# Adaptive max pooling on one core: 63 consecutive rows for each partition, a nine-row ring, 48 KB load runs and 9 KB store runs

## The chip, the cores and the metric

One core of a Trainium2 chip; no other core of it ran. The metric is the device time of one execution in microseconds (us). "Before" is the kernel before the change, "changed" the kernel after it. The profiled span is about 2 us shorter than the reported time (336.9 against 339 for before). "Packet records" are the start, duration and size of every DMA packet, as the trace holds them.

## The reference

32 x 256 rows of 4096 floats (134.2 MB) become 32 x 256 rows of 256 floats (8.4 MB). As 4096 is a multiple of 256, each output is the maximum of 16 neighbours.

```python
for i in range(output_size):                       # 256
    start = int(i * length / output_size)          # 16 i
    end = int((i + 1) * length / output_size)
    result[:, :, i] = np.max(x[:, :, start:end], axis=-1)
```

## The kernel before

There are 8192 rows, 64 for each of the 128 partitions. Tile `n` takes 256 consecutive rows, two for each partition, so a partition reads one run of 32 KB and the next partition's run follows directly. Three such tiles rotate. SyncE issues the loads, VectorE reduces, ScalarE issues the first stores, and the last 16 stores of the body are held back and put on SyncE's queue between and behind the last loads.

```python
xt = xf.rearrange("(n p r) (o w) -> n p r o w", p=P, r=R, w=W)   # R = 2
ot = of.rearrange("(n p r) m -> n p (r m)", p=P, r=R)
...
for n in range(n_body):                                          # 30
    t = in_pool.tile([P, R, O, W], fp32, tag="in")               # bufs=3
    nc.sync.dma_start(out=t, in_=xt[n])                          # 4 MB, 32 KB a partition
    o = new_out()
    for r in range(R):
        nc.vector.reduce_max(out=o[:, r * O : (r + 1) * O], in_=t[:, r], ...)
    out_tiles[n] = o
    if n >= defer_start:
        deferred.append(n)                                       # held back
    else:
        nc.scalar.dma_start(out=ot[n], in_=o)                    # 256 KB, 2 KB a partition
...  # two rows loaded whole, two rows in four pieces of 4 KB a partition, held stores in between
```

Of the kernel before, what the change touches and what calls it, by code (L numbers as in the profile page):

```python
# [1 line left out]

# [4 lines left out]


@with_exitstack  # L10
def kernel(
    ctx: ExitStack,
    tc: tile.TileContext,
    x: bass.AP,
    output_size: bass.AP,
    out: bass.AP,
):
    nc = tc.nc

    B, C, L = x.shape  # L20
    O = int(output_size)
    assert L % O == 0, (L, O)
    W = L // O

    P = nc.NUM_PARTITIONS

    xf = x.flatten_outer_dims()
    of = out.flatten_outer_dims()
    rows = xf.shape[0]
    assert rows % P == 0  # L30

    fp32 = mybir.dt.float32

    R = 2
    IN_BUFS = 3
    CHUNKS_PER_ROW = 4
    N_CHUNK_ROWS = 2
    N_FULL_ROWS = 2
    DEF_A = 6
    DEF_B = 5  # L40
    DEF_C = 5

    while R > 1 and rows % (P * R) != 0:
        R //= 2
    nprow = rows // P
    nmacro = nprow // R
    n_chunks = CHUNKS_PER_ROW if O % CHUNKS_PER_ROW == 0 else 1
    oc = O // n_chunks

    n_tail_prow = min(N_CHUNK_ROWS + N_FULL_ROWS, nprow)  # L50
    n_chunk_prow = min(N_CHUNK_ROWS, n_tail_prow)
    n_tail_macro = -(-n_tail_prow // R)
    n_body = nmacro - n_tail_macro
    tail_start_prow = n_body * R
    n_defer = min(DEF_A + DEF_B + DEF_C, max(n_body - 1, 0))

    xt = xf.rearrange("(n p r) (o w) -> n p r o w", p=P, r=R, w=W)
    ot = of.rearrange("(n p r) m -> n p (r m)", p=P, r=R)

    in_pool = ctx.enter_context(tc.tile_pool(name="inpool", bufs=IN_BUFS))  # L60
    out_pool = ctx.enter_context(
        tc.tile_pool(name="outpool", bufs=min(nmacro, n_defer + 5))
    )

    out_tiles = {}
    deferred: list[int] = []

    def new_out():
        return out_pool.tile([P, R * O], fp32, tag="out", name="o")

    def emit_deferred(k):
        for _ in range(k):
            if deferred:
                m = deferred.pop(0)
                nc.sync.dma_start(out=ot[m], in_=out_tiles[m])  # L75

    defer_start = n_body - n_defer
    for n in range(n_body):
        t = in_pool.tile([P, R, O, W], fp32, tag="in")
        nc.sync.dma_start(out=t, in_=xt[n])  # L80
        o = new_out()
        for r in range(R):
            nc.vector.reduce_max(  # L83
                out=o[:, r * O : (r + 1) * O],
                in_=t[:, r],
                axis=mybir.AxisListType.X,
            )
        out_tiles[n] = o
        if n >= defer_start:
            deferred.append(n)  # L90
        else:
            nc.scalar.dma_start(out=ot[n], in_=o)

    emit_deferred(DEF_A)

    o = None
    last_n = nmacro - 1
    for q in range(tail_start_prow, nprow):
        n, r = divmod(q, R)
        if r == 0 or o is None:  # L100
            o = new_out()
            out_tiles[n] = o
        if q == nprow - n_chunk_prow:
            emit_deferred(DEF_B)
        if q < nprow - n_chunk_prow:
            tr = in_pool.tile([P, 1, O, W], fp32, tag="inrow", bufs=2)
            nc.sync.dma_start(out=tr, in_=xt[n][:, r : r + 1])
            nc.vector.reduce_max(  # L108
                out=o[:, r * O : (r + 1) * O],
                in_=tr[:, 0],  # L110
                axis=mybir.AxisListType.X,
            )
        else:
            for c in range(n_chunks):
                tl = in_pool.tile(
                    [P, oc, W], fp32, tag="inchunk", bufs=2 * n_chunks
                )
                nc.sync.dma_start(
                    out=tl, in_=xt[n][:, r, c * oc : (c + 1) * oc, :]
                )  # L120
                nc.vector.reduce_max(  # L121
                    out=o[:, r * O + c * oc : r * O + (c + 1) * oc],
                    in_=tl,
                    axis=mybir.AxisListType.X,
                )
        if r == R - 1 and n != last_n:
            nc.scalar.dma_start(out=ot[n], in_=o)

    emit_deferred(len(deferred))

    nc.scalar.dma_start(out=ot[last_n], in_=out_tiles[last_n])


# [1 line left out]
_INS = ['x', 'output_size']  # L135
_OUTS = [((32, 256, 256), 'float32')]
#: Inputs that are plain numbers.
_NUMBERS = {'output_size': 256}


# [26 lines left out]
```

## Time and profile before

| What | Before | Where it is read |
|---|---|---|
| time, median of 3 first runs | 339.17 us | runs |
| span | 336.9 us | page |
| VectorE busy | 281.0 us, 83% | page, part 1 |
| bytes moved | 142.6 MB | page, parts 2 and 3 |
| DMA share from 20 to 280 us | 1.00 to 1.01 | windows |
| one row reduced | 4.41 us | groups of instructions |

From the page of before, its lines on VectorE, on the DMA engines (busy tenths in 40 slices, then GB/s of each slice), on packets and on the queues (q1 is SyncE's, q10 ScalarE's):

```profile
span 336.9 us, 241 instructions
...
DVE 281.0 (83%) x70; POOL 0.2 (0%) x4
...
DMA  7999999999999999999999999999999999999997
GB/s 311 436 436 441 417 454 406 454 409 454 426 430 430 436 428 434 430 430 435 429 438 432 436 432 436 436 436 428 424 436 428 436 412 436 429 414 427 405 414 275
DMA packets 10370, 142.63 MB, mean 423 GB/s; under 512 B 1152, under 2 KB 1152, under 8 KB 6272
...
q1 hardware_dynamic: 8064, 138.42, 96.1%
q10 hardware_dynamic: 2304, 4.20, 3.2%
```

The 1152 packets under 512 B are 4-byte ones, 16 for each of the 72 DMAs, which report that a DMA is done; they are called semaphore packets below. The DMA line stands at nine tenths or more in every slice but the first and the last. VectorE is well used too, but not all the time.

Two stretches of before in the windows view. The columns are the stretch, its length, VectorE's busy time with its instruction count, GpSimd's, the TensorE clock, the DMA share and GB/s:

```profile
core 0: us, DVE busy (x) POOL busy (x), PEclk, DMA share, GB/s
20.00:160.00 140.00, 118.67 (x28) 0.00 (x0) 1.00 1.01 431
185.00:280.00 95.00, 85.25 (x21) 0.00 (x0) 1.00 1.00 431
```

A DMA share of 1.00 means that the 16 engines had, as good as always, a packet in hand. It can read more, for two reasons: the view adds up whole packets that start in the stretch, and a packet overlaps the next one slightly. With the packets clipped to the stretch the two shares are 1.006 and 1.003.

The group of whole-row reduces of before (busy us, mean ns of one, then the idle time in front of them and who ended it):

```profile
L83 DVE TENSOR_REDUCE o<-t 128x256 f32<-128x4096 f32 x60 | 262.4, 4414 | 50.5 <-DMA t<-in_x_dram 50.5
```

And a piece of before's chain of waits, with its shares by line (start us, length us, what):

```profile
by line: DMA t<-in_x_dram 60.0%; DVE o L83 23.4%; DMA out_dram<-o 10.7%; DMA tl<-in_x_dram 2.8%; DVE o L121 0.7%; SPq L75 0.5%; SPq L80 0.3%; issue 0.3%; DVEq L83 0.0%
...
64.09 8.76 DVE o L83 x2
72.85 0.02 issue
72.87 22.19 DMA t<-in_x_dram
```

The chain gives VectorE 24% of the span. It is easy to read this as "a quarter of the time is compute on the critical path". It isn't: the load that follows a reduce was free to be issued only when the reduce freed its buffer, but two other loads were still outstanding at that moment, and the DMA engines did not run dry. The 22 us that the chain shows for a load of 4 MB is more than twice what 4 MB takes at 431 GB/s (9.7 us): the rest is waiting in the queue.

### The profile page before, as it was taken

To read this page: it belongs to the slowest core of one execution; us is meant where nothing else is said; L and a number is where in the kernel's file an instruction comes from. 1 tells how busy PE (TensorE), PEld (TensorE's weight loads), DVE (VectorE), ACT (ScalarE), POOL (GpSimd) and SP (SyncE) were. 2 spreads that over 40 slices of the span, in tenths; PEclk is the share of its full clock that TensorE was granted. 3 is DMA by queue.
4 is the path that set the end of the run, shared out by engine and by line. 5 is a ranking of instruction groups with operands and counts; after the bars stand their busy time and mean duration, and the time that the engine had idled before them with its cause. 6 is when DMAs were issued, how large, how long until landed. Compare 5 with 4: busy or idle time off the path is not lost.

```text
span 336.9 us, 241 instructions
## 1 busy us (share of the span) xinstructions
DVE 281.0 (83%) x70; POOL 0.2 (0%) x4
## 2 busy tenths in 40 slices
DVE  0488988888988889888899888888988888898895
POOL 0000000000000000000000000000000000000000
DMA  7999999999999999999999999999999999999997
GB/s 311 436 436 441 417 454 406 454 409 454 426 430 430 436 428 434 430 430 435 429 438 432 436 432 436 436 436 428 424 436 428 436 412 436 429 414 427 405 414 275
DMA packets 10370, 142.63 MB, mean 423 GB/s; under 512 B 1152, under 2 KB 1152, under 8 KB 6272
## 3 DMA queue, kind: packets, MB, share of 16 engines
q1 hardware_dynamic: 8064, 138.42, 96.1%
q10 hardware_dynamic: 2304, 4.20, 3.2%
q14 instruction: 2, 0.02, 0.0%
HBM read 134.22 MB, written 8.39 MB: 423 GB/s over the span
## 4 chain that ended last, share of the span: by engine, by line
DMA 74%; DVE 24%; SPq 1%; issue 0%; DVEq 0%
DMA t<-in_x_dram 60%; DVE o L83 23%; DMA out_dram<-o 11%; DMA tl<-in_x_dram 3%; DVE o L121 1%; SPq L75 1%; SPq L80 0%; DVEq L83 0%
## 5 line engine op out<-in xcount | busy, mean ns | idle before, releaser
L83 DVE TENSOR_REDUCE o<-t 128x256 f32<-128x4096 f32 x60 | 262.4, 4414 | 50.5 <-DMA t<-in_x_dram 50.5
L121 DVE TENSOR_REDUCE o<-tl 128x64 f32<-128x1024 f32 x8 | 9.8, 1220 | 1.0 <-DMA tl<-in_x_dram 0.6
L108 DVE TENSOR_REDUCE o<-tr 128x256 f32<-128x4096 f32 x2 | 8.8, 4420 | 1.0 <-DMA tr<-in_x_dram 0.9
L148 POOL MEMSET const-bfloat16-1.0<- 128x1 bf16 x1 | 0.1, 102 | 0.0
L148 POOL MEMSET const-uint8-127<- 128x1 uint8 x1 | 0.1, 101 | 0.0
L148 POOL MEMSET const-float32-0.0<- 128x1 f32 x1 | 0.1, 99 | 0.2 <-issue 0.2
L148 POOL MEMSET const-float32-1.0<- 128x1 f32 x1 | 0.1, 98 | 0.0
## 6 DMA issues: line engine op xcount, KB each, us to landing
t<-in_x_dram SPq DMA_DIRECT2D x30, 4096.0 KB, 21.5
out_dram<-o ACTq DMA_DIRECT2D x16, 256.0 KB, 16.1
out_dram<-o SPq DMA_DIRECT2D x16, 256.0 KB, 14.0
tr<-in_x_dram SPq DMA_DIRECT2D x2, 2048.0 KB, 16.4
tl<-in_x_dram SPq DMA_DIRECT2D x8, 512.0 KB, 9.2
```

Source lines behind the costliest of these rows:

```text
L75: nc.sync.dma_start(out=ot[m], in_=out_tiles[m])
L83: nc.vector.reduce_max(out=o[:, r * O : (r + 1) * O], in_=t[:, r], axis=mybir.AxisListType.X,)
L108: nc.vector.reduce_max(out=o[:, r * O : (r + 1) * O], in_=tr[:, 0], axis=mybir.AxisListType.X,)
L121: nc.vector.reduce_max(out=o[:, r * O + c * oc : r * O + (c + 1) * oc], in_=tl, axis=mybir.AxisListType.X,)
L148: nc = _bacc.Bacc("TRN2", target_bir_lowering=False, num_devices=1)
```

## The change

Its intent is longer runs and fewer packets. Each partition owns 63 consecutive rows; with three rows a load it reads runs of 48 KB, and with nine rows a store it writes runs of 9 KB. The price is that neighbouring partitions now read 63 x 16 KB = 1008 KB apart. The last 128 rows, one for each partition, are handled at the end. A ring of nine rows takes the place of three two-row buffers.

```diff
-    R = 2
-    IN_BUFS = 3
...
+    RING = 9
+    G = 63
+    STORE = 9
+    LOAD = 3
+    LATE = [3, 2, 2, 1, 1]
+    HELD = 4
+    PIECES = 4
...
-    xt = xf.rearrange("(n p r) (o w) -> n p r o w", p=P, r=R, w=W)
-    ot = of.rearrange("(n p r) m -> n p (r m)", p=P, r=R)
...
+    main = G * P
+    xg = xf[0:main].rearrange("(p s r) (o w) -> s p r o w", p=P, r=STORE, w=W)
+    og = of[0:main].rearrange("(p s r) m -> s p (r m)", p=P, r=STORE)
+    xl = xf[main:rows].rearrange("p (o w) -> p o w", w=W)
+    ol = of[main:rows]
...
+    for g in range(G // STORE):
+        o = outs[g % len(outs)]
+        sizes = LATE if g == G // STORE - 1 else [LOAD] * (STORE // LOAD)
+        r = 0
+        for n in sizes:
+            at = n_read % RING
+            nc.sync.dma_start(out=ring[:, at : at + n], in_=xg[g][:, r : r + n])
+            for i in range(n):
                 nc.vector.reduce_max(
-                    out=o[:, r * O + c * oc : r * O + (c + 1) * oc],
-                    in_=tl,
+                    out=o[:, (r + i) * O : (r + i + 1) * O],
+                    in_=ring[:, at + i],
                     axis=mybir.AxisListType.X,
                 )
+            n_read += n
+            r += n
+        if g < G // STORE - 1 - HELD:
+            nc.scalar.dma_start(out=og[g], in_=o)
+        else:
+            held.append((og[g], o))
...  # the last row in PIECES loads and reduces
+    for dst, src in held:
+        nc.sync.dma_start(out=dst, in_=src)
+    nc.scalar.dma_start(out=ol, in_=last_out)
```

More of the change, by code (lines that the diff above doesn't have):

```diff
@@ L18 @@
     nc = tc.nc
+    P = nc.NUM_PARTITIONS
+    fp32 = mybir.dt.float32
     B, C, L = x.shape
@@ L23 @@
     W = L // O
-    P = nc.NUM_PARTITIONS
     xf = x.flatten_outer_dims()
@@ L29 @@
     rows = xf.shape[0]
-    assert rows % P == 0
-    fp32 = mybir.dt.float32
-    R = 2
-    IN_BUFS = 3
-    CHUNKS_PER_ROW = 4
-    N_CHUNK_ROWS = 2
-    N_FULL_ROWS = 2
-    DEF_A = 6
-    DEF_B = 5
-    DEF_C = 5
-    while R > 1 and rows % (P * R) != 0:
-        R //= 2
-    nprow = rows // P
-    nmacro = nprow // R
-    n_chunks = CHUNKS_PER_ROW if O % CHUNKS_PER_ROW == 0 else 1
-    oc = O // n_chunks
-    n_tail_prow = min(N_CHUNK_ROWS + N_FULL_ROWS, nprow)
-    n_chunk_prow = min(N_CHUNK_ROWS, n_tail_prow)
@@ L52 @@
-    n_tail_macro = -(-n_tail_prow // R)
-    n_body = nmacro - n_tail_macro
-    tail_start_prow = n_body * R
-    n_defer = min(DEF_A + DEF_B + DEF_C, max(n_body - 1, 0))
-    xt = xf.rearrange("(n p r) (o w) -> n p r o w", p=P, r=R, w=W)
-    ot = of.rearrange("(n p r) m -> n p (r m)", p=P, r=R)
-    in_pool = ctx.enter_context(tc.tile_pool(name="inpool", bufs=IN_BUFS))
-    out_pool = ctx.enter_context(
-        tc.tile_pool(name="outpool", bufs=min(nmacro, n_defer + 5))
-    )
-    out_tiles = {}
@@ L66 @@
-    deferred: list[int] = []
-    def new_out():
-        return out_pool.tile([P, R * O], fp32, tag="out", name="o")
-    def emit_deferred(k):
-        for _ in range(k):
-            if deferred:
-                m = deferred.pop(0)
-                nc.sync.dma_start(out=ot[m], in_=out_tiles[m])
-    defer_start = n_body - n_defer
-    for n in range(n_body):
-        t = in_pool.tile([P, R, O, W], fp32, tag="in")
-        nc.sync.dma_start(out=t, in_=xt[n])
-        o = new_out()
-        for r in range(R):
-            nc.vector.reduce_max(
-                out=o[:, r * O : (r + 1) * O],
-                in_=t[:, r],
-                axis=mybir.AxisListType.X,
-            )
-        out_tiles[n] = o
-        if n >= defer_start:
-            deferred.append(n)
-        else:
-            nc.scalar.dma_start(out=ot[n], in_=o)
@@ L94 @@
-    emit_deferred(DEF_A)
-    o = None
-    last_n = nmacro - 1
-    for q in range(tail_start_prow, nprow):
-        n, r = divmod(q, R)
-        if r == 0 or o is None:
-            o = new_out()
-            out_tiles[n] = o
-        if q == nprow - n_chunk_prow:
-            emit_deferred(DEF_B)
-        if q < nprow - n_chunk_prow:
-            tr = in_pool.tile([P, 1, O, W], fp32, tag="inrow", bufs=2)
-            nc.sync.dma_start(out=tr, in_=xt[n][:, r : r + 1])
-            nc.vector.reduce_max(
-                out=o[:, r * O : (r + 1) * O],
-                in_=tr[:, 0],
-                axis=mybir.AxisListType.X,
-            )
-        else:
-            for c in range(n_chunks):
-                tl = in_pool.tile(
-                    [P, oc, W], fp32, tag="inchunk", bufs=2 * n_chunks
-                )
-                nc.sync.dma_start(
-                    out=tl, in_=xt[n][:, r, c * oc : (c + 1) * oc, :]
-                )
+    assert rows == 64 * P
@@ new lines @@
+    RING = 9
[5 more added lines that the diff above has]
+    PIECES = 4
+    pool = ctx.enter_context(tc.tile_pool(name="pool", bufs=1))
+    ring = pool.tile([P, RING, O, W], fp32, tag="ring", name="ring")
+    outs = [
+        pool.tile([P, STORE * O], fp32, tag=f"out{i}", name=f"out{i}")
+        for i in range(G // STORE - 1)
+    ]
+    last_out = pool.tile([P, O], fp32, tag="lastout", name="lastout")
+    main = G * P
+    xg = xf[0:main].rearrange("(p s r) (o w) -> s p r o w", p=P, r=STORE, w=W)
@@ new lines @@
+    og = of[0:main].rearrange("(p s r) m -> s p (r m)", p=P, r=STORE)
+    xl = xf[main:rows].rearrange("p (o w) -> p o w", w=W)
+    ol = of[main:rows]
+    n_read = 0
+    held = []
+    for g in range(G // STORE):
[6 more added lines that the diff above has]
+            for i in range(n):
@@ L121 @@
                 nc.vector.reduce_max(
-                    out=o[:, r * O + c * oc : r * O + (c + 1) * oc],
-                    in_=tl,
+                    out=o[:, (r + i) * O : (r + i + 1) * O],
+                    in_=ring[:, at + i],
                     axis=mybir.AxisListType.X,
                 )
-        if r == R - 1 and n != last_n:
-            nc.scalar.dma_start(out=ot[n], in_=o)
-    emit_deferred(len(deferred))
-    nc.scalar.dma_start(out=ot[last_n], in_=out_tiles[last_n])
+            n_read += n
@@ new lines @@
+            r += n
[3 more added lines that the diff above has]
+            held.append((og[g], o))
+    at = n_read % RING
+    oc = O // PIECES
+    for c in range(PIECES):
+        cut = slice(c * oc, (c + 1) * oc)
+        nc.sync.dma_start(out=ring[:, at, cut], in_=xl[:, cut])
+        nc.vector.reduce_max(
+            out=last_out[:, cut], in_=ring[:, at, cut], axis=mybir.AxisListType.X
+        )
+    for dst, src in held:
+        nc.sync.dma_start(out=dst, in_=src)
```

## The prediction

> **What bounds the kernel now.** The memory traffic, and nothing else. The profile's page gives a span of 336.9 us in which the DMA engines are busy in nine tenths or more of every slice but the first and last; its DMA queues moved 142.6 MB (134.2 MB read, 8.4 MB written, as they must be). The windows view shows a DMA share of 1.00 to 1.01 from 20 to 280 us, at 431 GB/s. The Trainium skill, "DMA: Bandwidth & Descriptors", section "Where 436 GB/s comes from", states 435.2 GB/s as the ceiling of the 16 ports; the trace agrees, it runs 1% below. VectorE is busy 281 us (83%): its wait in front of the loads (50.5 us) is slack, not cost. The chain of waits alternates 22 us of load and 8.76 us of reduce, but that is the buffer loop closing behind a full queue: in the packet records the first packet starts about 2 us after the span's start, the last ends about 1 us before its end, and all 16 engines are busy between, except some 1.3 us of imbalance in the last 5 us.
>
> So the floor of any rearrangement is about 142.6 MB / 435.2 GB/s = 327.7 us (an estimate from that page), plus 3 us of start and end and 2.3 us between span and reported time: 333 us. Over 2% faster (below 332.4 us) isn't there.
>
> **What the change does.** The arithmetic is the same: 62 whole-row reduces of 4.41 us become 63, eight quarter-row ones of 1.22 us become four. The ring is three slots of three rows instead of three of two, still triple buffering. Loads: 3840 packets of 32 KB become 2432 of 48 KB (plus 256 of 32 KB); 1024 pieces of 4 KB become 512. Stores: 4096 packets of 2 KB become 896 of 9 KB and 128 of 1 KB. 72 DMAs become 35, so 1152 semaphore packets become 560.
>
> Costs, read from the trace: loads alone ran at 432.4 GB/s (185 to 280 us), loads with 2 KB stores at 431.7, and the small-packet end at 386 to 420. Above pure payload a 32 KB packet costs about 2 to 4 ns and a 2 KB packet about 5 (80 ns start to start, against 75). Per engine I estimate: stores 256 x 5 ns shrink to a quarter, -0.9 us; long loads -0.2 us; 4 KB pieces -0.1 us; semaphores 37 x 9 ns, -0.3 us. All of it is on the critical path, since the queue is it. Sum -1.5 us; a slightly better end could give 0.5 more.
>
> Will the queue stay full? A slot of three rows is freed 13.2 us after it lands, a load lasts about 14.6 us, and another whole load is queued: yes. At the end, VectorE finishes about 10.6 us after the last load, but four held stores (10.9 us) and the fifth cover it.
>
> **The row pitch.** Partitions now lie 1008 KB apart, not 32 KB. The same page, section "Latency and other measured facts", reports losses for large power-of-two pitches and none once padded by 4 KiB. 1008 KB is no power of two, so I expect no loss. No run here has shown it.
>
> **Prediction.** 337.4 us, 80% range 335.6 to 341. Faster by over 2%: 0.01; within: 0.88; slower: 0.11.
>
> **Right if**: DMA share stays 1.00 in the middle at 431 to 434 GB/s; packets near 5040; VectorE's mean per row stays 4.41 us; no idle DMA in the last 15 us.
>
> **Wrong if**: the long pitch makes 48 KB packets last over 1.82 us (then GB/s in mid-span falls, evenly); the held stores fail to cover VectorE's end (idle DMA near the end); or engines drift apart and end unevenly.

## The result, and the profile after

The changed kernel took 336.94 us (median of 4 runs, 336.87 to 337.29) beside 338.95 for before: ratio 0.9941, 95% interval 0.9925 to 0.9957. Two more series gave 0.9954 and 0.9945. The mean of the three is 0.9947, that is 1.8 us of about 338.8: a real gain of half a per cent, which counts as the same time at a threshold of 2%.

The same lines of the changed kernel's page:

```profile
span 335.1 us, 174 instructions
...
DVE 278.8 (83%) x67; POOL 0.2 (0%) x4
...
DMA  9999999999999999999999999989999999999997
GB/s 358 393 458 422 434 452 411 450 378 421 463 452 399 424 452 462 399 458 411 446 452 393 458 452 405 458 387 463 452 399 458 405 452 426 434 431 399 407 434 317
DMA packets 5041, 142.62 MB, mean 426 GB/s; under 512 B 560, under 2 KB 688, under 8 KB 1200
...
q1 hardware_dynamic: 4608, 140.12, 97.4%
q10 hardware_dynamic: 432, 2.49, 1.8%
```

Half the packets (10370 to 5041), the same bytes, the same full DMA line; the mean rate over the span rises from 423 to 426 GB/s. The two queues' packets fill 99% of the engines' span in both kernels (q1 and q10 together). The single slices now swing between 378 and 463 GB/s; that is not unsteady traffic but counting: a packet's bytes go to the slice in which it starts, and a 48 KB packet is long.

The two stretches of the changed kernel, columns as above:

```profile
20.00:160.00 140.00, 120.96 (x29) 0.00 (x0) 1.00 1.00 432
185.00:280.00 95.00, 86.23 (x20) 0.00 (x0) 1.00 1.00 432
```

The group of whole-row reduces, and the chain's shares with a piece of it:

```profile
L65 DVE TENSOR_REDUCE out<-ring 128x256 f32<-128x4096 f32 x63 | 274.3, 4412 | 50.8 <-DMA ring<-in_x_dram 50.8
```

```profile
by line: DMA ring<-in_x_dram 61.6%; DVE out L65 31.3%; issue 2.6%; DVE lastout L82 1.3%; DVEq L119 1.3%; DVEq L65 0.0%
...
62.08 13.08 DVE out L65 x3
75.17 0.02 issue
75.18 33.67 DMA ring<-in_x_dram
```

A row costs VectorE 4.41 us as before. The chain now gives VectorE a third of the span, although the kernel became faster and VectorE's work did not change: a larger load step makes each loop through a buffer longer, and the chain follows the buffers. From the packet records of the trace, the first packet starts 1.75 us after the span's start in both kernels, and the last ends 1.2 us before its end in both; the stretch between shrinks from 333.96 to 332.21 us. So the whole gain lies between the first and the last packet: most of it in how long the full queue takes for the same bytes, and a part at the end, where the engines finish unevenly. In the last 5 us before the last packet ends, an engine is idle for 1.27 us on average in before, and for 0.70, 1.12 and 1.03 us in the three profiles of the changed kernel.

### The profile page after: what moved, and what is told of

It reads as the page before. It is cut to its first block, busy times and chain, and to the rows that moved or that the text cites. A ratio compares the mean times of both kernels' runs of the same rounds, so it can differ in the third digit from the quotient of the medians. Undisturbed runs are those within 1.5% of the kernel's fastest.

```text
span 335.1 us, 174 instructions
## 1 busy us (share of the span) xinstructions
DVE 278.8 (83%) x67; POOL 0.2 (0%) x4
## 2 busy tenths in 40 slices
DMA packets 5041, 142.62 MB, mean 426 GB/s; under 512 B 560, under 2 KB 688, under 8 KB 1200
## 4 chain that ended last, share of the span: by engine, by line
DMA 62%; DVE 33%; issue 3%; DVEq 1%
DMA ring<-in_x_dram 62%; DVE out L65 31%; DVE lastout L82 1%; DVEq L119 1%; DVEq L65 0%
## 5 line engine op out<-in xcount | busy, mean ns | idle before, releaser
L65 DVE TENSOR_REDUCE out<-ring 128x256 f32<-128x4096 f32 x63 | 274.3, 4412 | 50.8 <-DMA ring<-in_x_dram 50.8
L82 DVE TENSOR_REDUCE lastout<-ring 128x64 f32<-128x1024 f32 x4 | 4.6, 1208 | 0.0
```

The lines of the kernel that those rows point to most:

```text
L65: nc.vector.reduce_max(out=o[:, (r + i) * O : (r + i + 1) * O], in_=ring[:, at + i], axis=mybir.AxisListType.X,)
L82: nc.vector.reduce_max(out=last_out[:, cut], in_=ring[:, at, cut], axis=mybir.AxisListType.X)
```

## The experiments

Each kernel ran beside before on the same chip, in three series on three chips; four to six executions of each. The diffs below are cut to their main lines ("..."). Differences to the changed kernel are taken between ratios to before, times 338.8 us; the 95% interval of each ratio is about 0.13% to each side, so such a difference is uncertain by some 0.6 us where it compares two series, and by less within one, where both ratios share the runs of before. The changed kernel itself ran in the first and third.

| Run | What is different | Time, us | Ratio to before (95%) | Against changed, us |
|---|---|---|---|---|
| after_again | nothing (control, series 1) | 337.29 | 0.9954 (0.9942 to 0.9966) | 0 |
| after_third | nothing (control, series 3) | 336.77 | 0.9945 (0.9933 to 0.9957) | 0 |
| pitch_block | 144 KB pitch | 336.80 | 0.9941 (0.9929 to 0.9954) | -0.4 |
| pitch_1mib | 1 MiB pitch | 340.09 | 1.0039 (1.0027 to 1.0051) | +2.9 |
| before_1mib | before, with 1 MiB pitch | 342.47 | 1.0109 (1.0095 to 1.0123) | (+3.7 against before) |
| store_1k | store runs of 1 KB | 340.05 | 1.0034 (1.0021 to 1.0047) | +2.7 |
| load_16k | load runs of 16 KB | 338.78 | 0.9996 (0.9984 to 1.0009) | +1.7 |
| load_1row | one row a load DMA | 339.89 | 1.0031 (1.0018 to 1.0043) | +2.9 |
| held_0 | no store held back | 342.64 | 1.0112 (1.0097 to 1.0128) | +5.6 |
| dve_extra | 26.5 us more VectorE work | 337.12 | 0.9951 (0.9938 to 0.9963) | +0.1 |
| lean | coarser last loads | 336.71 | 0.9937 (0.9924 to 0.9951) | -0.3 |
| block_lean | 144 KB pitch and coarser last loads | 336.61 | 0.9936 (0.9923 to 0.9948) | -0.3 |

All outputs were correct. For load_16k, held_0 and dve_extra, which ran without a control, the comparison is with 0.9947.

### The controls

> The changed kernel once more, as the control of this series. My theory (the queue is full in both, fewer packets save about 2 us): ratio to the kernel before 0.994, within 0.0015. Rival (the first ratio was luck of one chip): 0.998 or more.

> The changed kernel a third time, as the control of this series: ratio to the kernel before 0.9945, within 0.0015.

0.9954 and 0.9945. Both intervals exclude 0.998, so the gain is not the luck of one chip; it is repeated within 0.0013.

### Is VectorE on the critical path? (dve_extra)

```diff
+    spare = pool.tile([P, O], fp32, tag="spare", name="spare")
...
+            if r == 0 and g < G // STORE - 1:
+                nc.vector.reduce_max(out=spare, in_=ring[:, at], axis=mybir.AxisListType.X)
```

> The changed kernel with one needless row reduce in each of the first six groups of nine rows, written to a spare buffer: 6 x 4.41 = 26.5 us more VectorE work, 305 us in all. Theory (VectorE has slack, the chain of waits misleads where it gives it a third of the span): the time grows by less than 0.5 us. Rival (the chain is right and reduces are on the critical path): 9 us (a third of it) to 26 us more.

The time stayed where it was (0.9951). From the page, and from the list of who waited for whom (waits in us, how often, the longest), of the kernel with the needless reduces:

```profile
span 335.9 us, 175 instructions
...
DVE 303.9 (90%) x73; POOL 0.2 (0%) x4
```

```profile
DVE out L66 <- DMA ring<-in_x_dram: 26.3, 9, 18.9
```

And the same wait in the changed kernel:

```profile
DVE out L65 <- DMA ring<-in_x_dram: 50.8, 19, 18.5
```

VectorE's busy time grew by 25 us to 90% of the span, and its wait for loads shrank by 24.5 us. The extra work was taken out of its own idle time. The chain's 33% for VectorE is thus slack, and not time that a faster VectorE would give back.

### What does a packet cost? (store_1k, load_16k)

Both pad rows in the buffer, so that a transfer of the same bytes, in the same number of DMAs, must be made of shorter runs.

```diff
-        pool.tile([P, STORE * O], fp32, tag=f"out{i}", name=f"out{i}")
+        pool.tile([P, STORE, O + 16], fp32, tag=f"out{i}", name=f"out{i}")
...
-            nc.scalar.dma_start(out=og[g], in_=o)
+            nc.scalar.dma_start(out=og[g], in_=o[:, :, 0:O])
```

> The changed kernel with output rows padded in the buffer, so that a store's run is 1 KB instead of 9 KB; same number of DMAs, 8064 packets of 1 KB in place of 896 of 9 KB. Theory (short stores cost by packet and the queue is full): 504 packets an engine at 43 to 46 ns against 56 at 343 ns, so 2.4 to 4 us longer than the changed kernel, that is as slow as or slower than the kernel before. Rival (store length doesn't matter, the gain came from elsewhere): under 0.7 us.

```diff
-    ring = pool.tile([P, RING, O, W], fp32, tag="ring", name="ring")
+    ring = pool.tile([P, RING, O * W + 16], fp32, tag="ring", name="ring")
...
-            nc.sync.dma_start(out=ring[:, at : at + n], in_=xg[g][:, r : r + n])
+            nc.sync.dma_start(out=ring[:, at : at + n, 0:L], in_=xg[g][:, r : r + n])
```

> The changed kernel with ring rows padded, so that a load's run is 16 KB instead of 48 KB; same number of DMAs. About 5120 more packets, 320 an engine. Theory (2 to 4 ns a packet): 0.6 to 1.3 us longer than the changed kernel. Rival (run length of loads is worth nothing at this size): under 0.4 us. Rival (run length is most of the gain): 2 us or more.

The packet lines of the two pages, short stores first, then short load runs:

```profile
DMA packets 12210, 142.62 MB, mean 422 GB/s; under 512 B 561, under 2 KB 8753, under 8 KB 9265
```

```profile
DMA packets 10161, 142.62 MB, mean 423 GB/s; under 512 B 560, under 2 KB 688, under 8 KB 1200
```

Short stores cost 2.7 us, inside the expected 2.4 to 4; short load runs 1.7 us, a little above the expected 0.6 to 1.3, with the rival of 2 us or more inside its uncertainty. 7168 more store packets are 448 an engine: 2.7 us / 448 = 6.0 ns each. 5120 more load packets are 320 an engine: 1.7 us / 320 = 5.2 ns each. Each is uncertain by about 1.5 ns. The packet records agree. The median packets of 1, 2, 9, 16, 32 and 48 KB last 46, 84, 347, 611, 1213 and 1815 ns, each 8 to 9 ns above 602 ns for 16 KB, and a packet overlaps the next by some 3 to 4 ns (a clipped share of 1.002 with packets of 1815 ns); from 180 to 270 us, where loads alone run, the changed kernel moves 433.0 GB/s and load_16k 429.8, which is some 6.7 ns for each packet more. So both directions charge about the same for a packet on top of its bytes, at the sizes tried; and either change, alone, takes back nearly all of the change's gain (load runs of 16 KB) or more than that (store runs of 1 KB).

### What does a DMA cost? (load_1row)

```diff
-    LOAD = 3
+    LOAD = 1
```

> The changed kernel with loads of one row each up to the last group, 54 DMAs of 16 KB runs in place of 18 of 48 KB. It differs from the run with padded ring rows only in the number of DMAs. Theory (a DMA costs one 9 ns semaphore packet an engine): 0.3 us longer than that run, 1.5 to 2 us longer than the changed kernel. Rival (each DMA costs the queue far more, a drain of 0.1 us or more): 4 us or more longer. Rival (a shorter load lets VectorE start 9 us sooner and that helps): faster than the padded run by 1 us or more.

```profile
DMA packets 10226, 142.63 MB, mean 422 GB/s; under 512 B 1136, under 2 KB 1264, under 8 KB 1776
```

It has the 16 KB runs of load_16k except in the last group, and 36 more DMAs. It took 0.35% longer than that run, 1.2 us, or about 33 ns a DMA. That is more than the 9 ns that a semaphore packet lasts in the trace and less than the rival's 0.1 us, so neither expectation held. The last group keeps its long runs, 32 packets an engine fewer than load_16k has, which the expectation overlooked; at 5.2 ns each this makes it 38 ns. The two runs stem from different series, so the figure is uncertain by half. The trace supports the lower part: in the packet records from 130 to 270 us of the span, where only loads run, 20 more DMAs left each engine 0.43 us less for bytes, some 22 ns each. The third theory, that VectorE's earlier start helps, falls: nothing got faster.

### Does the pitch matter? (pitch_block, pitch_1mib, before_1mib)

```diff
# pitch_block
-    xg = xf[0:main].rearrange("(p s r) (o w) -> s p r o w", p=P, r=STORE, w=W)
-    og = of[0:main].rearrange("(p s r) m -> s p (r m)", p=P, r=STORE)
+    xg = xf[0:main].rearrange("(s p r) (o w) -> s p r o w", p=P, r=STORE, w=W)
+    og = of[0:main].rearrange("(s p r) m -> s p (r m)", p=P, r=STORE)
# pitch_1mib: 64 rows a partition, the last of them handled last
...
+    xa = xf.rearrange("(p g) (o w) -> p g o w", p=P, w=W)
+    oa = of.rearrange("(p g) m -> p (g m)", p=P)
...
# before_1mib
-    xt = xf.rearrange("(n p r) (o w) -> n p r o w", p=P, r=R, w=W)
+    xt = xf.rearrange("(p n r) (o w) -> n p r o w", p=P, r=R, w=W)
...  # the same for ot
```

> The changed kernel with the old kind of layout: each group of nine rows per partition is one contiguous block, so partitions lie 144 KB apart instead of 1008 KB; run lengths, DMAs and order as in the changed kernel. Theory (the pitch neither helps nor hurts at 1008 KB): within 0.3% of the changed kernel, mid-span rate 433 GB/s. Rival 1 (the long pitch costs something that hides a larger gain of the long runs): 0.5% or more faster than the changed kernel, with fewer long packets in its first 100 us. Rival 2 (the long pitch is what gained): back at the kernel before, ratio 0.998 to 1.002.

> The changed kernel with 64 rows for each partition, so that the pitch is exactly 1 MiB; the 64th row is the one that comes last. Theory (a power-of-two pitch hurts, the 63 avoids it): slower than the changed kernel by 3 to 15%, 48 KB packets over 1.9 us throughout. Rival (the one-way load stream has room to spare at this pitch): within 0.3% of the changed kernel, 48 KB packets at 1.815 us.

> The kernel before with only its row assignment changed, 64 consecutive rows for each partition, so runs of 32 KB and 2 KB stay but the pitch is 1 MiB. If a 1 MiB pitch hurts: slower than the kernel before by 3 to 15%, as the changed kernel at 1 MiB is. If it doesn't: within 0.3% of the kernel before.

At 144 KB the kernel is 0.4 us faster than at 1008 KB in this series, and equal in the other (block_lean against lean, below): no difference that was repeated. (Within the first series the runs hardly overlap, 336.61 to 336.85 us against 336.79 to 337.42.) Rival 1, a gain of 0.5% or more, falls, and so does rival 2. At exactly 1 MiB it loses 2.9 us, more than the whole change gains, and before loses 3.7 us by the same layout. The theory (a power of two hurts) has the right sign; its size, 3 to 15%, and its "throughout" were wrong. The windows of the control and then of the 1 MiB kernel show where the time goes:

```profile
core 0: us, DVE busy (x) POOL busy (x), PEclk, DMA share, GB/s
0.00:35.00 35.00, 14.76 (x4) 0.20 (x4) 1.00 0.96 407
35.00:110.00 75.00, 64.33 (x16) 0.00 (x0) 1.00 1.01 433
110.00:145.00 35.00, 29.37 (x7) 0.00 (x0) 1.00 1.02 437
145.00:280.00 135.00, 121.86 (x29) 0.00 (x0) 1.00 1.00 431
```

```profile
0.00:35.00 35.00, 13.07 (x3) 0.20 (x4) 1.00 0.97 388
35.00:110.00 75.00, 65.36 (x15) 0.00 (x0) 1.00 1.00 432
110.00:145.00 35.00, 27.66 (x7) 0.00 (x0) 1.00 1.01 426
145.00:280.00 135.00, 121.85 (x29) 0.00 (x0) 1.00 1.00 432
```

The DMA share stays near 1.00 in both, so the queue is as full; but bytes flow more slowly in the first 35 us (388 against 407 GB/s) and from 110 to 145 us (426 against 437), and about equally fast elsewhere. These two stretches make (19/407 + 11/437) x 35 us = 2.5 us of the 2.9. Such a difference must not be read from this view alone: it counts a packet's bytes where the packet starts, and one 48 KB packet more on each engine is 22 GB/s in 35 us. With each packet's bytes spread over its duration, the rates are 374 against 400 GB/s in the first stretch and 423 against 431 from 110 to 145 us, so the reading stands. Here are the long load packets of five kernels; "slow" is more than 2% above the usual duration, "excess" is what all packets took beyond that duration, for each engine:

| Kernel | Long packets | Median, ns | Mean, ns | Slow ones | Excess, us |
|---|---|---|---|---|---|
| before, 32 KB | 3840 | 1213 | 1217.1 | 22 | 0.98 |
| before_1mib, 32 KB | 3840 | 1213 | 1227.6 | 158 | 3.51 |
| after_again, 48 KB, 1008 KB pitch | 2432 | 1815 | 1825.7 | 85 | 1.63 |
| pitch_block, 48 KB | 2432 | 1815 | 1825.1 | 60 | 1.54 |
| pitch_1mib, 48 KB | 2432 | 1815 | 1839.2 | 162 | 3.68 |

At 1 MiB the median packet is as fast as ever. A few dozen packets at a time are slow, in bursts: 2.5 us of the excess lies in the first 30 us, when all engines have started together, and 0.8 us between 120 and 140 us. The Trainium skill, "DMA: Bandwidth & Descriptors", section "Latency and other measured facts", reports that large power-of-two pitches lose bandwidth and that a pad of 4 KiB restores it, and infers that streams in lock step meet in the same memory channels. The burst at the common start fits that inference, and with 16 KB off the pitch the excess of the first 30 us is 0.7 to 0.9 us (0.7 in before). But in before_1mib most of the added excess comes later, 1.3 us between 30 and 50 us, and the mechanism itself was not shown here. Both 1 MiB kernels also put their stores 64 KB apart. In pitch_1mib the first store packet comes at 66.8 us, so the first burst is of the loads alone; in before_1mib stores run from 26 us, and what part their pitch has was not tested.

### Do the held stores cover the end? (held_0, lean, block_lean)

```diff
# held_0
-    HELD = 4
+    HELD = -1
# lean
-    LATE = [3, 2, 2, 1, 1]
-    PIECES = 4
+    LATE = [3, 3, 2, 1]
+    PIECES = 1
```

> The changed kernel with no store held back: each goes out as soon as its group is reduced. Theory (held stores cover the 10.6 us by which VectorE trails the last load): the end is bare and the time grows by 6 to 10 us. Rival (the held stores don't matter, the queue has slack there): within 1 us.

> The changed kernel with the last loads cut less: 3, 3, 2 and 1 rows instead of 3, 2, 2, 1, 1, and the last row in one load instead of four. VectorE trails the last load and held stores cover it, so the fine cut should buy nothing: theory 0.1 to 0.4 us faster than the changed kernel (28 packets an engine fewer, four semaphores). Rival (the fine cut is needed for the end): 1 us or more slower.

> The two together: contiguous nine-row blocks (144 KB pitch) and the coarser end. If the small gain of the 144 KB pitch (0.5 us) was real, it is 0.3 to 0.6 us faster than the coarser end alone and about 0.7 us faster than the changed kernel; if it was noise, it equals the coarser end alone within 0.2 us.

The last stretches of the changed kernel, then those of the kernel that holds nothing back:

```profile
core 0: us, DVE busy (x) POOL busy (x), PEclk, DMA share, GB/s
320.00:330.00 10.00, 9.57 (x6) 0.00 (x0) 1.00 1.01 429
330.00:335.00 5.00, 0.00 (x0) 0.00 (x0) 1.00 0.62 255
335.00:341.00 6.00, 0.00 (x0) 0.00 (x0) 1.00 0.00 0
```

```profile
320.00:330.00 10.00, 10.00 (x4) 0.00 (x0) 1.00 0.96 397
330.00:335.00 5.00, 5.00 (x3) 0.00 (x0) 1.00 0.11 47
335.00:341.00 6.00, 3.23 (x3) 0.00 (x0) 1.00 0.46 183
```

With no store held, the DMA share falls to 0.11 from 330 to 335 us, while VectorE is busy all of that time: the engines wait for the last maxima. The cost was 5.6 us, just under the expected 6 to 10. I had used VectorE's lag behind the last load as planned for the changed kernel; in that kernel the traces show 9.7 us (last load packet at 319.9, last reduce done at 329.6), but with stores sent early the last loads are slowed by a store between them (296.0 to 306.7 us; last load packet at 330.7) and VectorE trails by 7.6 us only.

Cutting the last loads less finely costs nothing (0.9937 against 0.9945 of the control, not told apart; by the packet records it saves 32 data packets an engine, not 28), so the fine cut is not needed where held stores cover the end. The rival (1 us or more slower) falls. block_lean has the lowest ratio, 0.9936, but it equals lean and is not told apart from the changed kernel: no run here clearly beats it.

## Why the prediction was right

- **What bounds the kernel: right.** The DMA share is 1.00 to 1.02 in mid-span in every kernel with held stores, and 26.5 us of needless VectorE work changed nothing that could be measured (+0.1 us). Packets (5041) and time for a row (4.41 us) came as predicted. The floor of about 333 us, an estimate made from the 435.2 GB/s of the Trainium skill's "Where 436 GB/s comes from", was not reached by any run; the best was 336.6.
- **Queue stays full, end is covered: right.** The DMA share is 1.01 from 320 to 330 us in the changed kernel. VectorE trailed the last load by 9.7 us, not 10.6. "No idle DMA in the last 15 us" was not met to the letter: by the packet records an engine is idle there for 0.6 to 1.0 us in the three profiles of the changed kernel, as against 1.0 us in before.
- **The sum: right in size, its terms less so.** With the unit costs that the experiments gave (no run put back the 2 KB stores or the 32 KB loads alone, so these are estimates):

| Term | Predicted, us | Measured unit cost x count, us |
|---|---|---|
| stores, 192 packets an engine fewer | -0.9 | 6.0 ns x 192 = -1.2 |
| long loads, 72 packets fewer | -0.2 | 5.2 ns x 72 = -0.4 |
| 4 KB pieces, 32 packets fewer | -0.1 | 5.2 ns x 32 = -0.2 |
| 37 DMAs fewer | -0.3 | 22 to 38 ns x 37 = -0.8 to -1.4 |
| slow long packets (excess 0.98 to 1.63) | 0 | +0.7 |
| uneven end (idle in the last 5 us) | up to -0.5, beside the sum | -0.2 to -0.6 |
| sum | -1.5 | -2.1 to -3.1 (time: -1.8) |

By this table the term that was mis-sized most is "semaphores 37 x 9 ns": a DMA in a full queue cost more than its semaphore packet lasts. But the sum overshoots the time, so the unit costs are probably too large together. Counted straight from the packet records, at the median duration of each size, each engine's packets shrink by 3.0 us, of which 1.1 us had been hidden by overlap: 1.9 us for packets and DMAs together. How it is shared between the two stays open.

The prediction left out a term: in the changed kernel some long packets are slow, 0.87 us of excess in the first 10 us (0.65 in before) and 0.61 us between 60 and 80 us of its first profile. The latter is where the first 9 KB stores run among the loads; the slow packets begin at 62.2 us, after the store was issued (60.7) and before its first packet (64.1). The stores of the second group, from 111 to 126 us, met no slow packet in two of three profiles (0.17 us in the other), and the contiguous layout has the slow stretch as well, so the pitch isn't its cause. What is stays open. This loss and the less uneven end partly cancel, so that the total came as near as it did is in part luck.

- **The row pitch: right as far as it went.** No loss could be told at 1008 KB. By the letter of "wrong if" the 48 KB packets did last too long, 1.826 us in the mean against 1.82; but the median is 1.815, the slow ones come in bursts and not evenly, and at 144 KB the mean is 1.825. The prediction rested on the skill's page for this; the experiments at 1 MiB show that the hazard was real and that one row less for each partition is what avoids it.

## What to carry to other kernels

When the DMA engines are full from first to last packet, count packets and DMAs, not waits: here a packet cost 5 to 7 ns an engine beyond its bytes and a DMA some 20 to 40 ns, so halving both bought half a per cent, while 26.5 us of work on the compute engine with slack made no difference. A chain of waits that alternates loads and compute doesn't show that compute costs time; add needless work to the engine and see. If a layout gives every partition a long stretch of memory, keep the pitch off a power of two (1 MiB is the one tried here), and keep enough finished stores back to cover the compute behind the last load.

## What the Trainium skill lacked or had wrong

- "DMA: Bandwidth & Descriptors", "Latency and other measured facts": its list of row pitches has 512 KiB and 2 MiB and up, for copies between HBM tensors. A 1 MiB pitch with load runs of 48 KB cost 0.85% (2.9 us of 337), with runs of 32 KB 1.1% (3.7 us of 339), most of it in bursts of slow packets (2.1 and 2.5 us more excess), with the median packet unchanged (1815 and 1213 ns). A pitch of 1 MiB less 16 KB cost 0.4 us in one comparison and nothing in the other. So the loss depends on more than the pitch: with 48 KB runs most of it came within 30 us of the engines' common start, with 32 KB runs about half of it between 30 and 50 us.
- The same page, "Why small descriptors are slow (HBM only)", puts the packet overhead at about 3 cycles and treats it as a matter of small descriptors. With the queue full, the runs give 5.2 to 6.0 ns a packet (uncertain by about 1.5), for load runs of 16 KB as well as for store runs of 1 KB.
- The same page, "Anatomy of one DMA", calls the semaphore write of about one cycle essentially free. In the traces a semaphore packet lasts 9 ns, and one DMA more in a full queue cost each engine some 22 to 38 ns. It is small, but 37 of them can be a good part of this change's gain (0.8 us at 22 ns). The section describes DMAs that GpSimd issues; here SyncE and ScalarE issue them.
- "HBM Reference", "Specifications (TRN2)", states about 425 GB/s for a core that streams alone: agreed, 423 and 426 GB/s over the span and 431 to 433 in mid-span.
- No page covers what slowed the long packets between 60 and 80 us, when the first 9 KB stores ran among 48 KB loads (0.5 to 0.6 us of excess in each of three profiles, 0 to 0.2 at the second group).
